# Token operands moved by 128 and 64 bytes in SBUF, a mask moved into the gates, two evacuations on another engine, one norm half a step earlier

## The chip, the cores and the metric

One core of one Trainium2 chip runs the whole program. The time is the device time of one execution in microseconds (us). Of three runs of the kernel before, the median is 1212.23 us (1207.42 to 1212.49). Engines are named as the profile names them: PE is TensorE's matrix multiply, PEld its weight load, DVE is VectorE, ACT is ScalarE, POOL is GpSimd, SP is SyncE, which here only issues DMAs.

## The reference, cut to what matters

A trunk of two layers on 512 tokens with 1024 channels, in float32. Each layer is a token mixer and a feed-forward network (FFN), each behind an RMS norm and added to the residual. The mixer of layer 0 is a convolution module, that of layer 1 a sparse attention with three branches per head.

```python
for i in range(2):
    h = rmsnorm(x, norm_mix[i])
    y = conformer_conv_module(h, ...) if i == 0 else nsa_attention(h, positions, ...)
    x = x + y
    h = rmsnorm(x, norm_ffn[i])
    gate, up = split(h @ w_in, 2)                 # 1024 -> 2 x 2816
    x = x + (silu(gate) * up) @ w_out             # 2816 -> 1024
```

In the attention the first branch looks at 31 compressed blocks of 32 tokens, the second at selected blocks (with 512 tokens all eight blocks are selected), the third at a window. Each branch's result is multiplied by a sigmoid gate:

```python
s_c = q @ k_cmp.T * scale
p_c = masked_softmax(s_c, cmp_end <= t)           # softmax of where(mask, s, -1e30), times mask
...
return g[0] * (p_c @ v_cmp) + g[1] * o_s + g[2] * o_w
```

Tokens 0 to 30 come before the end of the first compressed block: their whole row of `mask` is false, so `p_c` is zero there.

## The kernel before

Channels lie on the 128 partitions, tokens along the free axis, in tiles of 128 x 512. Each large product is made in float32r from halves: a float32 operand is split into a rounded high half and the rest, and high times high, high times low and low times high are added up in PSUM. A weight unit of 128 x 1024 comes by DMA into `wr`, ACT copies it to `wh`, DVE subtracts to `wl`. Names ending in h and l are such halves. In the profile nearly all instructions carry L136, the line of the helper that records them, so they are told apart by tile names.

The stages in order of time: conv module, first matmuls `pp<-hh,wh`, a convolution partly on PE (`cpe`) and partly on DVE, and an output product `pp<-a,wh` with the token tiles `a`; FFN of layer 0; projections, scores and outputs of the attention, ending in `pp<-oh,wh` and `pp<-ol,wh`; FFN of layer 1.

**The FFN.** The first channels are plain products of 512 columns. For the other 17 pairs of gate and up tiles per layer (function `pair`) the kernel uses seven products of half size in place of eight (Strassen's scheme in Winograd's form): `operand` combines the token tiles into `bh` and `bl` once, and for each pair the weights are combined: POOL starts two DMAs per pair into `S` (the second adds while it writes), adds `wr` to it, and `s_part` splits the sums into `sh` and `sl`. `product` then runs 4 x 3 matmuls with 256 columns each: the weights (`wh`, `wl`, `sh`, `sl`) are loaded into PE, the token half `bh` or `bl` streams. So a pair is 84 matmuls, and all pairs are 2 x 17 x 84 = 2856. The output product is `st<-ah,wh` and its like, with 512 columns.

**Where tiles lie.** Pools on the left side of SBUF are stacked upwards, those opened with `side="right"` downwards, so a small tile put on the right moves all right tiles that are opened after it. `EDGE` (24 floats) and `APART` (16 floats) are such tiles. By the addresses of the built program, the streamed tile starts this far from the weights that it meets, modulo 256 bytes: 64 for `pp<-hh` and `pp<-hl`, `st<-ah` and `st<-al`, `st<-bh` and `st<-bl`, and `pp<-oh`; 128 for `pp<-ol`; 192 for `pp<-a`. In `pv<-wh,hh` the roles are exchanged: the tokens `hh` are loaded as weights and `wh` or `wl` streams; there the distance is 192, with 256 or 304 columns.

**The attention.** `v_half(1, ...)` makes the window branch's values, four groups of 128 tokens in two PSUM banks, beside the first scores; `v_evac` copies them to SBUF, scaled by each token's norm. Then 16 steps follow (8 head pairs, two branches each). A step computes eight score tiles `S` (PE), their row maximum with the causal mask (DVE, `Pm,mx<-S`), the exponential and its sum (ACT), divides and multiplies by the gate (`weigh` on POOL, `Pm<-Pm,sm,gates`), transposes the result of the step before (`T`, PE, copied to `t` by DVE or ACT), and multiplies the one before that with the values (`O`). PE, DVE and ACT run in the order written here; for work that belongs beside the steps, the table `FILL` names what is run in each step's middle and end (`run_fill`, two entries a step; `+` joins several). `P1.0` to `P1.5` are the compressed branch's six parts for one pair of heads: `soft_a` (maximum, subtraction, exponential of the scores `sc`), `soft_b`, `soft_c` (row sum `cl`, its reciprocal, times the gate, times `sc`), `trans` (transposes to `pct`). The first pair's parts stand in `V_BESIDE` instead, beside the `pv` products. `n4` to `n7` multiply a query tile `qraw` by its norm, which PE spreads over the partitions (`bc<-qys,er`) in a PSUM bank of the same pool of three as `T` and `pct`.

Of the kernel before, what the change touches and what calls it, by code (L numbers as in the profile page):

```python
# [10 lines left out]
F32 = mybir.dt.float32  # L11
# [4 lines left out]
ALU = mybir.AluOpType  # L16
# [3 lines left out]
P = 128  # L20
T = 512
D = 1024
NK = 8
# [3 lines left out]
TAPS = 31  # L27
# [16 lines left out]
C_CMUL = C_CADD + 256  # L44
# [43 lines left out]
}  # L88
V_BESIDE = (
    (("w r12", "st0", "p2m", "sABCD a1"), ("w sa sb", "t1", "r13 c1", ""), ("w", "", "", "")),  # L90
    (("ga", "w", "s0", "s1 b1"), ("", "s2 s3 w", "gb s4 l", "s5 st1"), ("s6 l", "s7 l", "sc cu", "")))
EVAC_V = ((1, 3), (1, 3))
V_BANK = (2, 3, 0, 1)
STK_P = (0,)

FILL = ("tr0 P1.0  P1.1 P1.2  P1.3 P1.4  - n4+P1.5+d3  k3+P2.0 n5  P2.1+d5 P2.2  P2.3 P2.4  k5 P2.5  n6 n7+P3.0  "
        "P3.1 P3.2  P3.3 P3.4  wd P3.5  w0 -  w1").split()
SQB = 4
Q2B = 4
# [9 lines left out]
OUT_N = 256  # L109
EDGE = 24  # L110
APART = 16


def _two_pi_pieces():
# [34 lines left out]
def trunk(ctx: ExitStack, tc: tile.TileContext, A, out):  # L149
    order = [False]  # L150
    nc = Engines(tc, order)
# [9 lines left out]
    def nm(s):  # L161
        cnt[0] += 1
        return f"{s}_{cnt[0]}"
# [30 lines left out]
    for z in QV_ORDER:  # L194
        if z < 8:
            add("nw_q", z, 1024)
        else:
            w = VW[z - 8]
# [77 lines left out]
    cx0 = ExitStack()  # L276
    cb = cx0.enter_context(tc.tile_pool(name="cb", bufs=1, side="right"))
    ph = cb.tile([P, NPH], F32, name="ph")
    wdw = cb.tile([P, NK * TAPS + EDGE], F32, name="wdw")[:, :NK * TAPS]
    wtab = cb.tile([P, len(PE_CONV) - LOADED, 320], F32, name="wtab")  # L280
    i16 = cb.tile([P, 16], F32, name="i16")
    cc = cst.tile([P, NCST], F32, name="cc")
# [503 lines left out]
    def ffn(acc, gnext, layer, between=None):  # L786
# [9 lines left out]
        with ExitStack() as cx:  # L796
# [2 lines left out]
            pm = cx.enter_context(tc.tile_pool(name="fpm", bufs=6, space=PSUM, reuse_waits="tile"))  # L799
            pa = cx.enter_context(tc.tile_pool(name="fpa", bufs=2, space=PSUM, reuse_waits="tile"))  # L800
            sx = ExitStack()
            sb = sx.enter_context(tc.tile_pool(name="sb", bufs=1, side="right", reuse_waits="tile"))
            sx.enter_context(tc.tile_pool(name="apart", bufs=1, side="right")).tile([P, APART], F32, name=nm("apart"))
            sw = sx.enter_context(tc.tile_pool(name="sw", bufs=1, side="right", reuse_waits="tile"))
            box = {}

# [123 lines left out]
            def bank():  # L930
                return pm.tile([P, T], F32, tag="pm", name=nm("st"))
# [82 lines left out]
            pss, w, ws = {0: bank()}, {0: next_w(False)}, {}  # L1014
# [41 lines left out]
            for m, b in OUT_ORDER[4:]:  # L1056
# [12 lines left out]
                else:  # L1069
                    n = OUT_N if m == NK - 1 else T  # L1070
# [32 lines left out]
    def nsa(acc, cosT, sinT, gnext):  # L1103
        cx = ExitStack()

        def pool(cxx, name, bufs, **kw):
            return cxx.enter_context(tc.tile_pool(name=name, bufs=bufs, **kw))
# [81 lines left out]
        sx = ExitStack()  # L1189
# [199 lines left out]
        def q_pair(p):  # L1389

            a = p // 2
            sc = qk.tile([P, 4, 2, 64], F32, tag="sc", name=nm("sc"), bufs=1)

            def move(jj):
                q = oT[2 * p + jj]
                box["q2", jj] = []
                for par in range(2):
                    hs = slice(par * 64, par * 64 + 64)
                    q2 = qk.tile([P, T], F32, tag="q2", name=nm("q2"), bufs=Q2B)
                    for half in range(2):  # L1400
                        nc.sync.dma_start(q2[half * 64:half * 64 + 64], q[hs])
                    box["q2", jj].append(q2)

            def stacks(jj):
                j = 2 * p + jj
                S2 = qk.tile([P, 1088], F32R, tag="S", name=nm("St"), bufs=3)
                for par in range(2):
                    ls = slice(64 - par * 64, 128 - par * 64)
                    q2 = box["q2", jj][par]
                    S = S2[:, par * T:par * T + T]  # L1410
                    if p > 0 and par in STK_P:
                        nc.gpsimd.tensor_copy(S, q2)
                        nc.gpsimd.tensor_tensor(S[ls], q2[ls], S[ls], ALU.subtract)
                    else:
                        nc.scalar.activation(S, q2, AF.Copy)
                        behind(lambda S=S, q2=q2, ls=ls: nc.vector.tensor_tensor(S[ls], q2[ls], S[ls], ALU.subtract))
                    qst[j, par] = S

            def scores(jj):
                q = oT[2 * p + jj]  # L1420
                ps = p2.tile([P, 4, 64], F32, tag="p2", name=nm("psc"))
                for t in range(4):
                    pe(nc.tensor.matmul(ps[:, t, :], q[:, t * P:(t + 1) * P], kcb[a], start=True, stop=True))
                nc.vector.scalar_tensor_tensor(
                    sc[:, :, jj, :], ps, -1.0,
                    cc[:, C_CADD:C_CADD + 256].rearrange("p (t n) -> p t n", t=4), ALU.mult, ALU.add)

            def soft_a():
                s3 = sc.rearrange("p t j (h n) -> p (t j h) n", h=2)
                m = qk.tile([P, 16 + APART], F32, tag="cm", name=nm("cm"), bufs=1)[:, :16]  # L1430
                nc.vector.tensor_reduce(m, s3, AX.X, ALU.max)
                nc.vector.tensor_tensor(s3, s3, m.unsqueeze(2).to_broadcast([P, 16, 32]), ALU.subtract)
                sf = sc.rearrange("p t j n -> p (t j n)")
                behind(lambda: nc.scalar.activation(sf, sf, AF.Exp))

            def soft_b():
                s5 = sc.rearrange("p t j (h n) -> p t (j h) n", h=2)
                nc.gpsimd.tensor_tensor(
                    s5, s5, cc[:, C_CMUL:C_CMUL + 128].rearrange("p (t n) -> p t n", t=4)
                    .unsqueeze(2).to_broadcast([P, 4, 4, 32]), ALU.mult)  # L1440

            def soft_c():
                s3 = sc.rearrange("p t j (h n) -> p (t j h) n", h=2)
                l = qk.tile([P, 16], F32, tag="cl", name=nm("cl"), bufs=1)
                nc.vector.tensor_reduce(l, s3, AX.X, ALU.add)
                nc.vector.tensor_scalar(l, l, 0.5, None, ALU.max)
                nc.vector.reciprocal(l, l)
                r0 = 2 * (p % 2)
                gv = gates[:, :, 8 * a:8 * a + 8].rearrange("p t (h r) -> p t r h", h=2)[:, :, r0:r0 + 2, :]
                lv = l.rearrange("p (t j h) -> p t j h", t=4, j=2)  # L1450
                nc.vector.tensor_tensor(lv, lv, gv, ALU.mult)
                nc.gpsimd.tensor_tensor(
                    s3, s3, l.unsqueeze(2).to_broadcast([P, 16, 32]), ALU.mult)

            def trans():
                pt = p2.tile([P, T], F32, tag="p2", name=nm("pct"))
                for t in range(4):
                    pe(nc.tensor.transpose(pt[:, t * P:(t + 1) * P], sc[:, t].rearrange("p j n -> p (j n)"), ident))
                ph = q3[1].tile([P, T], F32R, tag="pch", name=nm("pch"))
                pl = q3[1].tile([P, T], F32R, tag="pcl", name=nm("pcl"))  # L1460
                nc.scalar.activation(ph, pt, AF.Copy)
                behind(lambda: nc.vector.tensor_tensor(pl, pt, ph, ALU.subtract))
                pcT[p] = (ph, pl)

            if p == 0:
                return move, scores, stacks, soft_a, soft_b, soft_c, trans
            return [lambda: (move(0), scores(0)), lambda: (stacks(0), scores(1)), lambda: (move(1), soft_a()),
                    lambda: (stacks(1), soft_b()), soft_c, trans]

        extra, bcs = {}, {}  # L1470

# [55 lines left out]
            extra[(f"q{j}", f"n{j}")[j > 3]] = lambda e=j + 6: (norm_mm(e), norm_x(e))  # L1527

        def first_pair():
            move, scores, stacks, soft_a, soft_b, soft_c, trans = q_pair(0)  # L1530
            extra.update(p0=lambda: scores(0), p1=lambda: scores(1), st0=lambda: stacks(0), st1=lambda: stacks(1),
                         p2m=lambda: move(1), sa=soft_a, sb=soft_b, sc=soft_c, tr0=trans)
            move(0)

        extra["m0q"] = first_pair
# [7 lines left out]
        for e in range(2, 14):  # L1543
# [7 lines left out]
            n = state["next"]  # L1551
# [18 lines left out]
        gates = ap_.tile([P, 4, 48], F32, name="gates")  # L1570
# [15 lines left out]
        def v_evac(hf, pst):  # L1586
            br = 1 + hf
            z = vf[br] = ap_.tile([P, 4, 256], F32, tag="w1v", name=f"v{br}", bufs=2)
            for t in range(4):
                ps = pst[t]  # L1590
                r1 = rt[:, t:t + 1]
                if t in EVAC_V[hf]:
                    nc.vector.tensor_scalar(z[:, t], ps[:, :256], r1, None, ALU.mult)
# [19 lines left out]
        def sigm_b():  # L1613
            g2 = gates.rearrange("p a b -> p (a b)")
            nc.vector.tensor_scalar(g2, g2, 1.0, None, ALU.add)
            nc.vector.reciprocal(g2, g2)

        extra["ga"] = sigm_a
        extra["gb"] = sigm_b
# [116 lines left out]
        N = len(us)  # L1736
        fill_ = list(FILL)
        U = {}
# [37 lines left out]
        pS.append(pool(ax, "apS2", 1, space=PSUM, **rw))  # L1776
        pO = pool(ax, "apO", 1, space=PSUM, **rw)
        ox = ExitStack()
        oha = pool(ox, "oha", 1, side="right", **rw)
        q3.append(pool(ax, "q3", 2, **rw))  # L1780
        box["q4"] = pool(ax, "q4", 2, **rw)
# [227 lines left out]
```

## Time and profile before

| | us |
|---|---|
| three runs: median, lowest, highest | 1212.23, 1207.42, 1212.49 |
| the profiled execution, its own time | 1214.0 |
| its span on the core | 1212.2 |
| PE busy in the span | 1192.2 |
| DVE, ACT, POOL busy | 791.0, 562.4, 369.9 |
| bytes moved by DMA | 154.25 MB |

The granted TensorE clock is 0.998 of full speed over the span. Matmuls are pipelined: a record of a matmul lasts longer than the distance to the next start, so a busy share near 1 says that PE's queue never ran dry, not how dense it ran. Below, the pitch of matmuls is taken from start to start. A bracket at a row's end gives the idle time of the engine before it and what ended it.

### The profile page before, as it was taken

What the parts mean: (1) busy time and instruction counts of PE and PEld (TensorE: products, weight loads), DVE (VectorE), ACT (ScalarE), POOL (GpSimd) and SP (SyncE); (2) the same over time, 40 slices, a digit from 0 to 9 for tenths busy, and PEclk for the clock granted to TensorE, in tenths of its full rate; (3) what the DMA queues carried; (4) which work ended last, traced back from release to release, by engine and by line L of the source; (5) the groups of instructions that cost most, each with busy time, mean ns of one, the idle gap of its engine ahead of it and who ended that gap; (6) DMA issues with size and microseconds to landing.
All of it is one profiled execution on the core that took longest, in us unless ns stands there. A gap on an engine that the chain in (4) does not pass through costs nothing.

```text
span 1212.2 us, 20771 instructions
## 1 busy us (share of the span) xinstructions
PE 1192.2 (98%) x8015; PEld 1022.9 (84%) x8015; DVE 791.0 (65%) x1453; ACT 562.4 (46%) x1048; POOL 369.9 (31%) x403
## 2 busy tenths in 40 slices
PE   9999899999999999999999999999999999999998
PEld 7888678799999988888779776778879999998887
DVE  7879686877776555334677778764597766656221
ACT  6212454455555443233335687773355555554111
POOL 1039022144443201102221577752213444410000
PEclk9999999999999999999999999999999999999999
DMA  9635326367777133244254211012626777723331
GB/s 363 251 107 141 80 90 198 112 157 183 185 188 178 59 105 96 97 146 113 80 140 125 52 37 36 18 36 85 181 100 160 186 192 187 181 75 99 113 114 44
DMA packets 81539, 154.25 MB, mean 127 GB/s; under 512 B 36128, under 2 KB 37024, under 8 KB 80672
## 3 DMA queue, kind: packets, MB, share of 16 engines
q1 hardware_dynamic: 66096, 109.04, 29.4%
q0 software_dynamic: 15344, 43.88, 15.3%
q8 instruction: 63, 1.03, 0.4%
q14 instruction: 36, 0.29, 0.1%
HBM read 139.37 MB, written 5.28 MB: 119 GB/s over the span
## 4 chain that ended last, share of the span: by engine, by line
PE 90%; DVE 5%; ACT 2%; issue 1%; POOL 1%; DVEq 0%; ACTq 0%
PE st L136 47%; PE pp L136 29%; PE cpe L136 2%; PE O L136 2%; PE S L136 2%; PE pv L136 2%; PE T L136 2%; ACT Pm L136 1%; DVE Pm L136 1%; DVE c L136 1%; POOL Pm L136 1%; DVE t L136 1%; DVE St L136 0%; PE psc L136 0%; DVE a L136 0%
## 5 line engine op out<-in xcount | busy, mean ns | idle before, releaser
L136 ACT ACTIVATE wh<-wr 128x1024 fp32r<-128x1024 f32 (+3 forms) x158 | 160.5, 1016 | 294.5 <-PE st L136 140.2
L136 DVE TENSOR_TENSOR wl<-wr,wh 128x1024 fp32r<-128x1024 f32 (+3 forms) x158 | 185.4, 1173 | 129.6 <-ACT wh L136 129.4
L136 PE MATMUL st<-bh,sl 128*128 128x256 f32 x680 | 190.3, 280 | 1.1 <-DVE sl L136 1.1
L136 PE MATMUL st<-bl,sh 128*128 128x256 f32 x680 | 190.1, 279 | 0.0
L136 PE MATMUL st<-bh,sh 128*128 128x256 f32 x680 | 189.7, 279 | 0.0
L136 PE MATMUL pp<-hh,wh 128*128 128x512 f32 x416 | 166.0, 399 | 1.6 <-ACT wh L136 1.0
L136 PE MATMUL pp<-hh,wl 128*128 128x512 f32 x416 | 163.2, 393 | 0.0
L136 PE MATMUL pp<-hl,wh 128*128 128x512 f32 x416 | 162.9, 392 | 0.0
L136 PE MATMUL st<-ah,wh 128*128 128x512 f32 x352 | 138.3, 393 | 0.0
L136 PE MATMUL st<-al,wh 128*128 128x512 f32 x352 | 137.7, 391 | 0.0
L136 PE MATMUL st<-ah,wl 128*128 128x512 f32 x352 | 137.3, 390 | 0.0
L136 PEld LDWEIGHTS st<-bh,sl 128*128 128x128 f32 x680 | 127.4, 187 | 1.5 <-DVE sl L136 1.5
L136 PEld LDWEIGHTS st<-bl,sh 128*128 128x128 f32 x680 | 127.8, 188 | 0.1
L136 PEld LDWEIGHTS st<-bh,sh 128*128 128x128 f32 x680 | 127.5, 188 | 0.1
L136 POOL TENSOR_TENSOR S<-S,wr 128x512 f32<-128x512 f32 x68 | 94.7, 1393 | 95.7 <-DMA wr<-fw_in 69.9
L136 POOL DMA_DIRECT2D S<-fw_x x68 | 60.4, 889 | 174.2 <-DVE sl L136 132.4
L136 DVE TENSOR_TENSOR sl<-S,sh 128x512 fp32r<-128x512 f32 x136 | 89.9, 703 | 33.4 <-ACT sh L136 33.3
L136 POOL TENSOR_SCALAR Pm<-Pm,sm,gates 128x512 f32<-128x512 f32 (+3 forms) x128 | 84.0, 670 | 49.8 <-DVE sm L136 31.5
L136 PEld LDWEIGHTS pp<-hh,wh 128*128 128x128 f32 x416 | 78.3, 188 | 23.2 <-issue 3.7
L136 PEld LDWEIGHTS pp<-hl,wh 128*128 128x128 f32 x416 | 78.3, 188 | 17.2 <-DVE hl L136 0.4
L136 PEld LDWEIGHTS pp<-hh,wl 128*128 128x128 f32 x416 | 78.2, 188 | 17.1 <-DVE wl L136 0.3
L136 POOL TENSOR_TENSOR acc<-acc,sq 128x512 f32<-128x512 f32 x18 | 31.7, 1763 | 192.4 <-ACT sq L136 179.0
(256 smaller groups left out, 2460.0 us busy)
## 6 DMA issues: line engine op xcount, KB each, us to landing
S<-fw_x POOLq DMA_DIRECT2D x68, 512.0 KB, 6.0
wr<-fw_in SPq DMA_DIRECT2D x46, 512.0 KB
wr<-fw_o SPq DMA_DIRECT2D x32, 512.0 KB
r<-fw_x SPq DMA_DIRECT2D x34, 256.0 KB
bd<-bands POOLq DMA_DIRECT2D x6, 1280.0 KB, 18.4
wr<-cw_in SPq DMA_DIRECT2D x14, 512.0 KB
wr<-fw_o SPq DMA_DIRECT2D x16, 384.0 KB
wr<-fw_s SPq DMA_DIRECT2D x8, 512.0 KB
```

The source lines that it names most:

```text
L136: z = f(*a, **kw)
```

## The change

Four edits. No constant of the computation differs.

1. Three spacers. `ASIDE` (32 floats) is put behind `wdw`, ahead of the FFN's pool of `bh` and `bl`, and added to the spacer behind that pool, so that `S`, `sh` and `sl` move by 256 bytes; 16 floats stand ahead of `oha`, the pool of `ol`. By the built addresses the distance modulo 256 bytes is now 192 for all 2856 matmuls that stream `bh` or `bl` (64 before), 64 for the 192 that stream `a` (192 before), and 64 for the 64 that stream `ol` (128 before). All other large products keep theirs.
2. `soft_b`, the product of `sc` with the mask on POOL, is gone, and so is the lower bound of 0.5 on the row sum `cl`. In their place one product multiplies the compressed branch's 16 gates of each token by the mask's first column, once.
3. `EVAC_V`: the second half's four evacuations `v<-pv` are all on ACT; two of them were on DVE.
4. `FILL`: `n4` moves from the end of step 4 to its middle, whose entry was empty.

```diff
-    (("w r12", "st0", "p2m", "sABCD a1"), ("w sa sb", "t1", "r13 c1", ""), ("w", "", "", "")),
+    (("w r12", "st0", "p2m", "sABCD a1"), ("w sa", "t1", "r13 c1", ""), ("w", "", "", "")),
...
-EVAC_V = ((1, 3), (1, 3))
+EVAC_V = ((1, 3), ())
...
-FILL = ("tr0 P1.0  P1.1 P1.2  P1.3 P1.4  - n4+P1.5+d3  ...
+FILL = ("tr0 P1.0  P1.1 P1.2  P1.3 P1.4  n4 P1.5+d3  ...
...
+ASIDE = 32
...
-    wdw = cb.tile([P, NK * TAPS + EDGE], F32, name="wdw")[:, :NK * TAPS]
+    wdw = cb.tile([P, NK * TAPS + EDGE + ASIDE], F32, name="wdw")[:, :NK * TAPS]
...
+            sx.enter_context(tc.tile_pool(name="aside", bufs=1, side="right")).tile([P, ASIDE], F32, name=nm("aside"))
             sb = sx.enter_context(tc.tile_pool(name="sb", bufs=1, side="right", reuse_waits="tile"))
-            ... .tile([P, APART], F32, name=nm("apart"))
+            ... .tile([P, APART + ASIDE], F32, name=nm("apart"))
...
-            def soft_b():
-                s5 = sc.rearrange("p t j (h n) -> p t (j h) n", h=2)
-                nc.gpsimd.tensor_tensor(
-                    s5, s5, cc[:, C_CMUL:C_CMUL + 128].rearrange("p (t n) -> p t n", t=4)
-                    .unsqueeze(2).to_broadcast([P, 4, 4, 32]), ALU.mult)
...
                 nc.vector.tensor_reduce(l, s3, AX.X, ALU.add)
-                nc.vector.tensor_scalar(l, l, 0.5, None, ALU.max)
                 nc.vector.reciprocal(l, l)
...
             nc.vector.reciprocal(g2, g2)
+            some = cc[:, C_CMUL:C_CMUL + 128].rearrange("p (t n) -> p t n", t=4)[:, :, :1]
+            nc.vector.tensor_tensor(gates[:, :, :16], gates[:, :, :16], some.to_broadcast([P, 4, 16]), ALU.mult)
...
+        pool(ox, "aside", 1, side="right").tile([P, APART], F32, name="aside")
         oha = pool(ox, "oha", 1, side="right", **rw)
```

How the instructions stand now, at three places. On DVE at the end of the value products, before the change (`cl` is `soft_c`'s row sum of the first pair, `St` a split of queries, `v` an evacuation, `Pm,mx` the row maximum of a score tile of step 1):

```order
L136 TENSOR_REDUCE cl_6938<-sc_6453 128x16
L136 TENSOR_SCALAR cl_6938<-cl_6938 128x16
L136 RECIPROCAL cl_6938<-cl_6938 128x16
L136 TENSOR_TENSOR cl_6938<-cl_6938,gates 128x16
L136 TENSOR_TENSOR St_6896<-q_643_6615,St_6896 64x512
L136 TENSOR_TENSOR St_6896<-q_644_6618,St_6896 64x512
L136 TENSOR_SCALAR v_6958<-pv_6773,rsy_5621 128x256
L136 TENSOR_SCALAR v_6958<-pv_6774,rsy_5621 128x256
L136 ISA Pm_6981,mx_6982<-S_6987,mask 128x512
```

and after:

```order
L137 TENSOR_REDUCE cl_6943<-sc_6458 128x16
L137 RECIPROCAL cl_6943<-cl_6943 128x16
L137 TENSOR_TENSOR cl_6943<-cl_6943,gates 128x16
L137 TENSOR_TENSOR St_6901<-q_644_6620,St_6901 64x512
L137 TENSOR_TENSOR St_6901<-q_645_6623,St_6901 64x512
L137 ISA Pm_6989,mx_6990<-S_6995,mask 128x512
L137 ISA mx_6990 128x1
```

The bound on `cl` (its TENSOR_SCALAR) and both evacuations `v` are gone from between the row sum and step 1's first maximum. On ACT there, two rows `v` became four, in the same place ahead of step 1's first exponential. On POOL in step 3, where the part `P1.3` of the second pair runs, before:

```order
L136 CAST St_7266<-q_726_7198 128x512
L136 TENSOR_TENSOR St_7266<-q_726_7198,St_7266 64x512
L136 TENSOR_TENSOR sc_7069<-sc_7069,cc 128x512
L136 TENSOR_SCALAR Pm_7221<-Pm_7221,sm_7223,gates 128x512
L136 TENSOR_SCALAR Pm_7221<-Pm_7221,sm_7223,gates 128x384
L136 TENSOR_SCALAR Pm_7221<-Pm_7221,sm_7223,gates 128x256
L136 TENSOR_SCALAR Pm_7221<-Pm_7221,sm_7223,gates 128x128
```

and after:

```order
L137 CAST St_7274<-q_727_7206 128x512
L137 TENSOR_TENSOR St_7274<-q_727_7206,St_7274 64x512
L137 TENSOR_SCALAR Pm_7229<-Pm_7229,sm_7231,gates 128x512
L137 TENSOR_SCALAR Pm_7229<-Pm_7229,sm_7231,gates 128x384
L137 TENSOR_SCALAR Pm_7229<-Pm_7229,sm_7231,gates 128x256
L137 TENSOR_SCALAR Pm_7229<-Pm_7229,sm_7231,gates 128x128
```

The product `sc<-sc,cc` no longer stands between the split of queries and the first weighing; the same happens in the two later pairs. On PE in step 4 before, the middle,

```order
L136 MATMUL T_7379<-cc,Pm_7221 128x128 x2
L136 MATMUL T_7379<-cc,Pm_7224 128x128 x2
L136 MATMUL T_7387<-cc,Pm_7221 128x128 x4
L136 MATMUL S_7397<-kst_6267,St_7144 128x512
L136 MATMUL S_7397<-kl_6268,St_7144 128x512
L136 MATMUL T_7402<-cc,Pm_7224 128x128 x4
```

and the end of the step:

```order
L136 MATMUL S_7422<-kst_6267,St_7144 128x256
L136 MATMUL S_7422<-kl_6268,St_7144 128x256
L136 MATMUL bc_7430<-qys_6825,er 128x512
L136 MATMUL pct_7433<-cc,sc_7069 128x128 x4
L136 MATMUL T_7447<-cc,Pm_7221 128x128 x4
L136 MATMUL T_7454<-cc,Pm_7224 128x128 x4
```

After, the middle of it:

```order
L137 MATMUL T_7385<-cc,Pm_7229 128x128 x2
L137 MATMUL T_7385<-cc,Pm_7232 128x128 x2
L137 MATMUL bc_7393<-qys_6829,er 128x512
L137 MATMUL T_7396<-cc,Pm_7229 128x128 x4
L137 MATMUL S_7406<-kst_6272,St_7152 128x512
L137 MATMUL S_7406<-kl_6273,St_7152 128x512
L137 MATMUL T_7411<-cc,Pm_7232 128x128 x4
```

`bc` now stands between the first four transposes of the step and the next four; on DVE its reader `qraw<-qraw,bc` moves with it, from behind the step's last maximum to ahead of the copy `t<-T` in the middle. Everything else stands in the order it had.

More of the change, by code (lines that the diff above doesn't have):

```diff
@@ L89 @@
 V_BESIDE = (
-    (("w r12", "st0", "p2m", "sABCD a1"), ("w sa sb", "t1", "r13 c1", ""), ("w", "", "", "")),
+    (("w r12", "st0", "p2m", "sABCD a1"), ("w sa", "t1", "r13 c1", ""), ("w", "", "", "")),
     (("ga", "w", "s0", "s1 b1"), ("", "s2 s3 w", "gb s4 l", "s5 st1"), ("s6 l", "s7 l", "sc cu", "")))
-EVAC_V = ((1, 3), (1, 3))
+EVAC_V = ((1, 3), ())
 V_BANK = (2, 3, 0, 1)
 STK_P = (0,)
-FILL = ("tr0 P1.0  P1.1 P1.2  P1.3 P1.4  - n4+P1.5+d3  k3+P2.0 n5  P2.1+d5 P2.2  P2.3 P2.4  k5 P2.5  n6 n7+P3.0  "
+FILL = ("tr0 P1.0  P1.1 P1.2  P1.3 P1.4  n4 P1.5+d3  k3+P2.0 n5  P2.1+d5 P2.2  P2.3 P2.4  k5 P2.5  n6 n7+P3.0  "
         "P3.1 P3.2  P3.3 P3.4  wd P3.5  w0 -  w1").split()
@@ L801, in ffn @@
             sx = ExitStack()
+            sx.enter_context(tc.tile_pool(name="aside", bufs=1, side="right")).tile([P, ASIDE], F32, name=nm("aside"))
             sb = sx.enter_context(tc.tile_pool(name="sb", bufs=1, side="right", reuse_waits="tile"))
-            sx.enter_context(tc.tile_pool(name="apart", bufs=1, side="right")).tile([P, APART], F32, name=nm("apart"))
+            sx.enter_context(tc.tile_pool(name="apart", bufs=1, side="right")).tile([P, APART + ASIDE], F32, name=nm("apart"))
             sw = sx.enter_context(tc.tile_pool(name="sw", bufs=1, side="right", reuse_waits="tile"))
@@ L1465, in q_pair @@
             if p == 0:
-                return move, scores, stacks, soft_a, soft_b, soft_c, trans
+                return move, scores, stacks, soft_a, soft_c, trans
             return [lambda: (move(0), scores(0)), lambda: (stacks(0), scores(1)), lambda: (move(1), soft_a()),
-                    lambda: (stacks(1), soft_b()), soft_c, trans]
+                    lambda: stacks(1), soft_c, trans]
         extra, bcs = {}, {}
@@ L1529, in first_pair @@
         def first_pair():
-            move, scores, stacks, soft_a, soft_b, soft_c, trans = q_pair(0)
+            move, scores, stacks, soft_a, soft_c, trans = q_pair(0)
             extra.update(p0=lambda: scores(0), p1=lambda: scores(1), st0=lambda: stacks(0), st1=lambda: stacks(1),
-                         p2m=lambda: move(1), sa=soft_a, sb=soft_b, sc=soft_c, tr0=trans)
+                         p2m=lambda: move(1), sa=soft_a, sc=soft_c, tr0=trans)
             move(0)
```

## The prediction

> **What bounds the kernel now.** I read the page's totals first, then the chain that ended last, then the costliest groups with their shapes, and then, since PE is never idle for long, the distances between matmul starts in the timeline of PE.
>
> ```profile
> span 1212.2 us, 20771 instructions
> PE 1192.2 (98%) x8015; PEld 1022.9 (84%) x8015; DVE 791.0 (65%) x1453; ACT 562.4 (46%) x1048; POOL 369.9 (31%) x403
> PE 90%; DVE 5%; ACT 2%; issue 1%; POOL 1%; DVEq 0%; ACTq 0%
> ```
>
> PE is busy for 98% of the span and 90% of the last chain. So only two things can move the time: how densely PE's matmuls follow each other, and the few places where PE waits.
>
> The groups that the change touches by address, and how often each occurs:
>
> ```profile
> L136 PE MATMUL st<-bh,sl 128*128 128x256 f32 x680 | 190.3, 280 | 1.1 <-DVE sl L136 1.1
> ...
> L136 PE MATMUL st<-bh,wl 128*128 128x256 f32 x272 | 76.0, 279 | 0.0
> ...
> L136 PE MATMUL pp<-a,wl 128*128 128x512 f32 x64 | 24.8, 395 | 0.0
> ```
>
> Three groups of 680 and three of 272 stream `bh` or `bl`: 2856. Their mean of 280 ns is longer than the distance to the next start, so it tells nothing of density; the pitch does. In the timeline of PE I took a stretch of each kind without a gap, its first and its last row:
>
> ```profile
> 320.84 0.28 PE L136 MATMUL st<-bh,sh 128*128 128x256 f32 x1
> ...
> 338.97 0.28 PE L136 MATMUL st<-bl,sh 128*128 128x256 f32 x1
> ...
> 660.12 0.28 PE L136 MATMUL pv<-wh,hl 128*128 128x256 f32 x1
> ...
> 661.48 0.28 PE L136 MATMUL pv<-wh,hl 128*128 128x256 f32 x1
> ...
> 461.66 0.39 PE L136 MATMUL st<-ah,wl 128*128 128x512 f32 x1
> ...
> 479.97 0.39 PE L136 MATMUL st<-al,wh 128*128 128x512 f32 x1
> ...
> 166.02 0.40 PE L136 MATMUL pp<-a,wl 128*128 128x512 f32 x1
> ...
> 181.42 0.40 PE L136 MATMUL pp<-a,wl 128*128 128x512 f32 x1
> ...
> 831.82 0.40 PE L136 MATMUL pp<-oh,wh 128*128 128x512 f32 x1
> ...
> 849.94 0.40 PE L136 MATMUL pp<-oh,wh 128*128 128x512 f32 x1
> ```
>
> With the starts counted between them, the pitches are:
> - `st<-bh` and kin, 256 columns, distance 64: 18.13 us over 154 starts, 117.7 ns;
> - `pv`, 256 columns, distance 192: 1.36 us over 12 starts, 113.3 ns;
> - `st<-ah` and kin, 512 columns, distance 64: 18.31 us over 80 starts, 228.9 ns;
> - `pp<-a`, 512 columns, distance 192: 15.40 us over 66 starts, 233.3 ns;
> - `pp<-oh` and `pp<-ol`, 512 columns, 64 and 128: 18.12 us over 78 starts, 232.3 ns.
>
> All five run at full clock with a weight load before every matmul. What differs is the place of their tiles: 512 columns do best at 64, 256 columns at 192.
>
> **The products in the FFN.** 2856 matmuls go from 64 to 192. The nearest row is `pv`: same 256 columns, same float32r, same order of two matmuls with one weight and a third with another, at 192. If the products take its pitch, each saves 117.7 - 113.3 = 4.4 ns, and all 2856 x 4.4 ns = 12.6 us. The other end comes from the 512 columns, where 192 is slower than 64 by 233.3 - 228.9 = 4.4 ns: 12.6 us lost. I take the gain, since its row has the same width and the same distance, while the other shares only the distance.
>
> The Trainium skill ("SBUF — State Buffer", section "Who interferes with whom") says that PE has two independent read ports, one for the streamed operand and one for weight loads, and that only the port pair shared by VectorE and GpSimd causes contention. By that rule the products would stay at 117.7 ns and this term would be zero; the pitches of `pp<-a` and `st<-ah`, 233.3 and 228.9 ns for the same shape, speak against it.
>
> **The two products of 512 columns.** `pp<-a` comes to 64: 192 x (233.3 - 228.9) = 0.8 us. `pp<-oh` and `pp<-ol` come to 64 throughout: 192 x (232.3 - 228.9) = 0.7 us. Together 1.5 us, with ends 0 and 1.5. The `cpe` matmuls stream `uf` against `bd`, which move together; a dozen more matmuls of the layer norm change their distance and are too few to count.
>
> **Does the FFN's supply keep up?** A pair of 84 products shrinks from 9.9 to 9.5 us. PE's wait for `sl` above is 1.1 us over the whole kernel. The transfers in the middle of the stage:
>
> ```profile
> core 0: us, PE busy (x) PEld busy (x) DVE busy (x) ACT busy (x), PEclk, DMA share, GB/s
> 300.00:340.00 40.00, 40.00 (x342) 40.00 (x341) 6.96 (x17) 4.53 (x12) 1.00 0.76 187
> ```
>
> The DMA engines are busy for 0.76; at the new pace it would be 0.79. I take no loss.
>
> **The end of the value products.** DVE, PE and ACT there:
>
> ```profile
> 672.68 0.54 DVE L136 TENSOR_SCALAR cl<-cl 128x16 f32<-128x16 f32 x1
> 673.89 2.14 DVE L136 TENSOR_TENSOR St<-q,St 64x512 fp32r<-64x512 f32 x2
> 675.96 0.86 DVE L136 TENSOR_SCALAR v<-pv,rsy 128x256 f32<-128x256 f32 x2
> 676.48 0.39 PE L136 MATMUL S<-kst,St 128*128 128x256 f32 x1 [1.97 <-DVE v L136]
> 677.48 0.39 PE L136 MATMUL S<-kst,St 128*128 128x256 f32 x1 [0.48 <-DVE mx L136]
> ...
> 673.74 0.48 ACT L136 ACTIVATE v<-pv,rsy 128x256 f32<-128x256 f32 x1 [0.22 <-PE pv L136]
> 677.46 0.72 ACT L136 ACTIVATE Pm<-Pm,mx 128x512 f32<-128x512 f32 x1 [3.24 <-DVE mx L136]
> ```
>
> PE waits 1.97 us until DVE has emptied a bank of `pv` behind two long splits, and then 0.48 us for the first row maximum. With all four on ACT the bank is free at about 674.2, ahead of PE's need; ACT's two more pieces of 0.48 us lie in its idle 3.24. Then the maximum is late next: DVE still does `St` first, but without the bound (0.54) and the two `v` (0.86), which overlap their neighbours a little, it comes 1.3 us earlier. So the gain is 1.3 us; the ends are 0, if the first exponential or its sum is late instead, and 2.45 (both waits). The added product on the gates is of the size of the other small ones on `gates`, some 0.25 us, once, and DVE idles longer just behind it:
>
> ```profile
> 667.54 0.25 DVE L136 TENSOR_SCALAR gates<-gates 128x192 f32<-128x192 f32 x1
> ...
> 670.75 0.42 DVE L136 CUSTOM_DVE_ANT_0 Pm<-S,mask 128x256 f32<-128x256 f32 x1 [0.48 <-PE S L136]
> ```
>
> **`soft_b`.** Four instructions on POOL. The first pair's lies in the value products, where PE does not wait for it. The other three look alike; this is the first of them, POOL and then PE and DVE:
>
> ```profile
> 700.76 1.29 POOL L136 TENSOR_TENSOR sc<-sc,cc 128x512 f32<-128x512 f32 x1
> 702.04 4.32 POOL L136 TENSOR_SCALAR Pm<-Pm,sm,gates 128x512 f32<-128x512 f32 x6
> ...
> 706.41 0.87 PE L136 MATMUL T<-cc,Pm 128*128 128x128 f32 x6 [0.58 <-POOL Pm L136]
> 707.97 0.66 PE L136 MATMUL T<-cc,Pm 128*128 128x128 f32 x4 [0.21 <-POOL Pm L136]
> ...
> 711.56 0.63 PE L136 MATMUL T<-cc,Pm 128*128 128x128 f32 x4 [0.99 <-DVE qraw L136]
> ...
> 707.33 0.69 DVE L136 COPY t<-T 128x512 f32<-128x512 f32 x1 [0.77 <-PE T L136]
> ...
> 710.74 0.67 DVE L136 TENSOR_TENSOR qraw<-qraw,bc 128x512 f32<-128x512 f32 x1
> ...
> PE T L136 <- POOL Pm L136: 2.3, 6, 0.6
> ```
>
> POOL runs without a gap from 700.76 on, and PE's transposes wait for it twice, 0.58 and 0.21 us; the last row (from the list of PE's waits between 640 and 800) gives 2.3 us for six such waits in all three places. 1.29 us less on POOL is more than either wait, so all 2.3 go; DVE idles 0.77 for the same cause and follows. Ends: 0, if DVE or ACT holds PE at the same places, and 3 x 1.29 = 3.9.
>
> **`n4`.** The wait of 0.99 us at 711.56 is for a PSUM bank that `bc` holds until DVE comes to `qraw`. In the step's middle that product (0.67 us) falls into DVE's idle 0.77 us, which edit 2 also shrinks, so part of it now delays the copy `t`. I take 0.7 us; ends -0.67 (all of it delays the copy and PE behind it) and 0.99.
>
> **The sum.** 12.6 + 1.5 + 1.3 + 2.3 + 0.7 = 18.4 us, 12.6 of it in the products. Against the profiled execution's own 1214.0 (span 1212.2) that is 1195.6; the median of the runs, 1212.23, lies 1.8 lower and would give 1193.8. I name 1195.
>
> **Rivals.**
> - The distance means nothing at 256 columns and `pv` is quicker for another reason: the small groups it runs in or the exchanged roles of tokens and weights. For it: the stretch is short, 12 starts against 154. Against it: `pp<-a` and `st<-ah` show that places matter. Then 1.5 + 1.3 + 2.3 + 0.7 = 5.8 us remain: 1206.4. The skill's rule of independent ports leads here too, and without the 1.5 us: 1207.9.
> - 192 is a bad distance for any stream, as 512 columns show: 2856 x 4.4 ns lost, less the other 5.8: 1212.2 + 12.6 - 5.8 = 1219. Against it stands the whole `pv` stretch. It decides from a pitch of 117.7 + 5800/2856 = 119.7 ns upwards, where the kernel gets slower than before.
> - The products' supply gets late, because 17 pairs in a row ask for more transfers per time; DMA, at 0.76, holds the pairs halfway. 6.3 us of the 12.6 are lost: 1200 to 1201.
>
> **How the numbers follow.** The sum 0.74, no effect at 256 columns 0.12, worse at 192 0.08, late supply 0.06. A measurement of this kernel can tell about 0.5%, 6 us: the first and the last are faster (0.80), the second is within it (0.12), the third slower (0.08). For the range, the sum's own lower end is 12.6 + 1.5 + 2.45 + 3.9 + 0.99 = 21.4, 1190.8 from the median, and 1189 with what single runs lie lower; upwards it takes in the late supply and the rival without effect, to 1208, which leaves out the slower rival and a little of each edge.
>
> **What the profile after would show.** Products right: the pitch of `st<-bh` in the middle of a pair near 113.3 ns, 154 starts in 17.5 us in place of 18.1, `pp<-a` and `pp<-oh` at 228.9. Supply wrong: idle before `st<-bh,sl` or `st<-bh,wh` above a few us, ended by DVE `sl` or `wl`. Evacuation right: no PE wait on `v` ahead of step 1, and the first `mx` 1.3 us earlier. `soft_b` right: PE's waits on POOL `Pm` gone. `n4` right: no PE wait on `qraw` in step 4, and no new one of that length on `t` or `pch`. The forecast is wrong if the pitch of the products stays at 117.7 or rises; no other term is large enough to save it.

## The result, and the profile after

The changed kernel takes 1202.52 us (median of 18 runs, 1195.52 to 1210.15) against 1213.15 us before (18 runs, 1205.91 to 1215.02): a ratio of the means of 0.9932, with a 95% interval from 0.9911 to 0.9954. By that interval it is faster by 5.6 to 10.8 us, where 18.4 us were worked out. The profiled execution took 1201.69 us. Three lines of its page, to be held against those of before:

```profile
span 1199.9 us, 20754 instructions
PE 1182.6 (99%) x8015; PEld 1015.9 (85%) x8015; DVE 794.6 (66%) x1448; ACT 562.1 (47%) x1050; POOL 363.4 (30%) x399
PE 92%; DVE 4%; ACT 2%; issue 1%; DMA 0%; SPq 0%; DVEq 0%; ACTq 0%
```

PE still bounds the kernel, and POOL has left the chain. From matmul start to matmul start, the two profiled executions differ by stage like this (us):

| stage | before | after | difference | forecast |
|---|---|---|---|---|
| `pp<-a`, first to last | 47.19 | 46.40 | -0.79 | -0.8 |
| products of the FFN, layer 0 | 171.62 | 171.61 | -0.01 | -6.3 |
| attention, last `pv` to last `O` | 141.76 | 136.88 | -4.89 | -4.3 |
| `pp<-oh`, `pp<-ol`, first to last | 44.44 | 43.83 | -0.61 | -0.7 |
| products of the FFN, layer 1 | 171.63 | 165.49 | -6.14 | -6.3 |

All other stages agree within 0.04 us, and the span is 12.3 us shorter. So one of two equal layers gained everything that was forecast for it and the other nothing. Two windows of 40 us, one in the products of layer 0 and one in those of layer 1, show it, first of before and then of after. The columns are the window, its length, PE's busy time with the number of matmuls `st` in it, the granted clock, the DMA share and GB/s.

```profile
320.00:360.00 40.00, 40.00 (x342) 1.00 0.77 189
1000.00:1040.00 40.00, 40.00 (x342) 1.00 0.76 186
```

```profile
320.00:360.00 40.00, 40.00 (x342) 1.00 0.75 188
1000.00:1040.00 40.00, 40.00 (x355) 1.00 0.79 194
```

A matmul of 0.28 us counts if any part of it lies in the window, so the pitch is (40 + 0.28)/n: 117.8 ns for 342 and 113.5 ns for 355. From the starts themselves it is 117.8 and 113.3 ns, and nothing between. Layer 0 runs at the one and layer 1 at the other, with the same code, the same distance of 192 and full clock in both. The timeline of PE after shows where the two layers part. These are the first wait for `sl` in layer 0 and in layer 1:

```profile
247.66 0.28 PE L137 MATMUL st<-bl,sh 128*128 128x256 f32 x1
248.47 0.39 PE L137 MATMUL st<-bh,sl 128*128 128x256 f32 x1 [0.54 <-DVE sl L137]
248.70 0.28 PE L137 MATMUL st<-bh,sh 128*128 128x256 f32 x1
...
249.52 0.28 PE L137 MATMUL st<-bl,sh 128*128 128x256 f32 x1
...
913.59 0.28 PE L137 MATMUL st<-bl,sh 128*128 128x256 f32 x1
914.41 0.39 PE L137 MATMUL st<-bh,sl 128*128 128x256 f32 x1 [0.53 <-DVE sl L137]
914.63 0.28 PE L137 MATMUL st<-bh,sh 128*128 128x256 f32 x1
...
915.44 0.28 PE L137 MATMUL st<-bl,sh 128*128 128x256 f32 x1
```

Both layers come into the wait at 117 to 118 ns. Seven starts after 248.70 layer 0 is at 249.52, 117 ns each. In layer 1 the single distances behind the wait are 222, 118, 122, 116, 114, 113 and then 113 to 114 ns: the faster pitch sets in within five matmuls of the wait. It holds for 93 distances, then comes a single one of 171 ns, and behind that it holds for 1307 more, up to twelve matmuls of 512 columns near the layer's end. This led to the theory that was tested: **the stream has two steady pitches, each interruption of PE chooses one, and the choice holds until the next interruption.** Its rivals were that the distance alone sets the pitch, and that something in layer 0 (its transfers, its weights) holds it back.

PE's waits in the attention after (640 to 800 us; total, times, longest) are those of before without `Pm` and `v`; `mx` has grown from 0.5 to 2.0 and `kl` from 0.5 to 0.9, and one on `sm` is new:

```profile
PE S L137 <- DVE mx L137: 2.0, 1, 2.0
PE T L137 <- DVE qraw L137: 1.0, 2, 0.7
PE S L137 <- DVE kl L137: 0.9, 1, 0.9
PE T L137 <- DVE sm L137: 0.4, 1, 0.4
```

### The profile page after: what moved, and what is told of

Its sections match the earlier page's. It is cut to its first block, busy times and chain, and to the rows that moved or that the text cites. A ratio compares the mean times of both kernels' runs of the same rounds, so it can differ in the third digit from the quotient of the medians.

```text
span 1199.9 us, 20754 instructions
## 1 busy us (share of the span) xinstructions
PE 1182.6 (99%) x8015; PEld 1015.9 (85%) x8015; DVE 794.6 (66%) x1448; ACT 562.1 (47%) x1050; POOL 363.4 (30%) x399
## 4 chain that ended last, share of the span: by engine, by line
PE 92%; DVE 4%; ACT 2%; issue 1%; DMA 0%; SPq 0%; DVEq 0%; ACTq 0%
PE st L137 47%; PE pp L137 29%; PE O L137 3%; PE S L137 3%; PE T L137 3%; PE cpe L137 2%; PE pv L137 2%; DVE c L137 1%; ACT Pm L137 1%; DVE Pm L137 1%; PE psc L137 0%; DMA x<-xT 0%; DVE a L137 0%; ACT wh L137 0%; ACT sh L137 0%
```

## The experiments

Pitches are means of start-to-start distances within a stretch; "fast" means 113.3 to 113.5 ns, "slow" 117.7 to 117.8 ns.

**The other edits without the spacers.**

```diff
-ASIDE = 32
 # both spacers of ASIDE and the one ahead of oha taken out
```

> Edits 2 to 4 without the spacers: distances 64, 192 and 128 as before the change. Theory lock (products run at 117.7 or 113.3 ns, chosen in each layer when PE comes out of its stall in the first pair and kept from there on; the distance only shifts the odds): times lie on levels 6.2 us apart, some 4.9 us under those of the kernel before: near 1208.5 with no layer fast, 1202.3 with one. Theory address alone (the distance sets the pitch, and layer 0 of the changed kernel is held at 117.7 by something of that layer): one level, 1208 to 1209, and no 113.3 anywhere in the products. Either way the stretch from the value products' end to the last O matmul is 136.9 us, as in the changed kernel, and pp<-a takes 47.2.

Measured: 1210.02 us (6 runs, 1208.55 to 1211.75) against 1213.67 (18 runs), ratio 0.997, interval 0.9958 to 0.9981. `pp<-a` and the output product are back at 47.20 and 44.46 us. Both layers run slow at distance 64, 171.6 us each, but layer 0 did not begin so. The timeline of PE in this kernel, the first and the 13th product, the next one and the wait:

```profile
246.77 0.28 PE L137 MATMUL st<-bh,wh 128*128 128x256 f32 x1
...
248.13 0.28 PE L137 MATMUL st<-bh,sh 128*128 128x256 f32 x1
248.24 0.28 PE L137 MATMUL st<-bl,sh 128*128 128x256 f32 x1
249.12 0.38 PE L137 MATMUL st<-bh,sl 128*128 128x256 f32 x1 [0.59 <-DVE sl L137]
```

From 246.77 to 248.13 are 12 distances of 113.3 ns, at 64 bytes. Behind the wait come 1401 distances of 117.8 ns on average, without a break. So the fast pitch exists at the old place too, and the wait ended it.

**The spacers alone.**

```diff
+ASIDE = 32
 # the three spacers of edit 1; edits 2, 3 and 4 undone
```

> The spacers alone, edits 2 to 4 undone: distances 192, 64, 64. Theory lock: levels near 1212, 1206 and 1199.5 (no, one or two layers fast), more often fast than the kernel before. Theory address alone: always layer 1 fast and layer 0 slow, one level near 1206. Either way pp<-a takes 46.4 and the oh products 43.8 us, and the stretch from the value products' end to the last O matmul is 141.8 us.

Measured: 1211.1 us (12 runs, 1205.5 to 1214.42) against 1213.67, ratio 0.997, interval 0.9955 to 0.9985. `pp<-a` gains 0.70 and the output product 0.61 us. In the profiled execution (1213.42 us) each layer runs fast for 93 matmuls behind the wait for `sl`, until, some 108 products into the layer, a distance of 166 ns (167 in layer 1) appears; from there on it is slow. The timeline there, with PE's weight loads (PEld) and ACT:

```profile
259.82 0.64 ACT L137 ACTIVATE c<-st 128x256 f32<-128x256 f32 x2
...
260.07 0.19 PEld L137 LDWEIGHTS st<-bh,sl 128*128 128x128 f32 x1
260.18 0.28 PE L137 MATMUL st<-bh,sl 128*128 128x256 f32 x1
260.23 0.19 PEld L137 LDWEIGHTS st<-bh,sh 128*128 128x128 f32 x1
260.29 0.33 PE L137 MATMUL st<-bh,sh 128*128 128x256 f32 x1
...
260.46 0.28 PE L137 MATMUL st<-bl,sh 128*128 128x256 f32 x1
```

An interruption of some 50 ns is enough. It is a wait for ACT, too short to be noted in a bracket: the product at 260.29 adds to a PSUM tile that ACT copies to `c` first, and the first of the two copies ends at 260.18. The load of that product's weights starts 57 ns after the matmul before it, where others start 2 to 5 ns after. In all 13 profiled executions whose first pair has the wait for `sl`, that copy starts 10.3 us behind the product that waited, at either pitch. A slow stream (17 layers) comes to the place 0.36 to 0.39 us after the copy has ended and shows no gap; a fast one (9 layers) comes 0.4 us earlier and has to wait, in each of the nine. Of these nine, seven were slow from there on (distances of 159 to 174 ns), and two stayed fast: layer 1 of the changed kernel (171 ns) and one at 64 bytes (193 ns). The times of the 12 runs, from 1205.5 to 1214.42, scatter by more than one layer's 6.2 us.

**Added interruptions.** In the next four kernels and two later ones, a matmul of another width, called a kick here, is put into the stream, once in two pairs or, in one kernel, in each of the first three. Its result goes to a spare PSUM tile and is used by nothing; the computation is otherwise complete.

```diff
+KICK = ((0, 512, 0, 448, 0, 384, 0, 352, 0, 320, 0, 304, 0, 288, 0, 272, 0),
+        (0, 480, 0, 416, 0, 368, 0, 336, 0, 312, 0, 296, 0, 280, 0, 264, 0))
...
                 product(b, w1, 1, 1, True, True)
+                if KICK[layer][n]:
+                    z = pa.tile([P, T], F32, tag="pa", name=nm("kick"))
+                    pe(nc.tensor.matmul(z[:, :KICK[layer][n]], w1[0][:, :P], bh[0][:, :KICK[layer][n]],
+                                        start=True, stop=True))
```

With 16 widths in the changed kernel (distance 192):

> The changed kernel with one extra matmul of another width (264 to 512 columns, its result unused) in the middle of every second pair of products, 16 in all. Theory lock: some of the 16 flip the pitch of all that follows between 117.7 and 113.3, both ways possible, and the pitch is the same within each stretch between two of them, in layer 0 too. Theory address alone: the pitch returns to the layer's own value (117.7 in layer 0, 113.3 in layer 1) behind each. The extra matmuls themselves cost 16 x 0.16 = 2.6 us.

The same 16 widths with the three spacers taken out (distance 64):

> The same 16 extra matmuls, spacers undone (distance 64). Theory lock: stretches at 113.3 appear at 64 as well, fewer or as many as at 192. Theory address alone: 117.7 in all stretches.

Measured: 1203.27 and 1211.78 us (one run each). Every stretch of 168 matmuls between two kicks has one pitch throughout. Windows of 18 us, now (18 + 0.28)/n: 161 or 162 is fast, 155 or 156 slow. First three stretches of layer 0 at 192 (behind 512, 448 and 384 columns):

```profile
262.20:280.20 18.00, 18.00 (x161) 1.00 0.79 202
281.50:299.50 18.00, 18.00 (x156) 1.00 0.80 205
301.50:319.50 18.00, 18.00 (x161) 1.00 0.83 203
```

and three of layer 1 at 64 (behind 368, 336 and 312 columns):

```profile
973.30:991.30 18.00, 18.00 (x161) 1.00 0.78 202
992.50:1010.50 18.00, 18.00 (x155) 1.00 0.76 205
1012.50:1030.50 18.00, 18.00 (x162) 1.00 0.78 202
```

At 192, 10 of 16 stretches are fast (behind 512, 384, 320, 304, 288, 272 in layer 0, and 416, 368, 312, 264 in layer 1); at 64, 2 of 16 (behind 368 and 312). Counted only where the stream was slow ahead of the kick, these are 6 of 8 and 2 of 14. Both layers have fast and slow stretches at 192, within the same supply, so neither the layer nor the transfers hold the pitch down; and both pitches occur at both distances, so the distance alone does not set it.

**One width again and again, at 192.** Layer 0 and layer 1 get these tables:

```diff
+KICK = ((0, 304, 0, 304, ...), (0, 320, 0, 320, ...))
```

> The changed kernel with an extra matmul of 304 columns in every second pair of layer 0 and of 320 in layer 1, eight each. Theory lock with a fixed outcome by width: as 304 and 320 columns both ended at 113.3 ns in the run with mixed widths, all 16 stretches behind them do, and the products take 2 x 162.5 us. Rival, lock with chance at each interruption: both pitches behind one and the same width, about 10 of 16 fast.

```diff
+KICK = ((0, 512, 0, 512, ...), (0, 288, 0, 288, ...))
```

> The same with 512 columns in layer 0 and 288 in layer 1. Fixed outcome by width: all 16 stretches at 113.3 ns. Fixed outcome by width and by the pitch before: 288 (fast to fast with mixed widths) keeps the state it finds fast, 512 (slow to fast) may alternate. Chance: about 10 of 16 fast, in no order.

Measured: 1208.29 and 1202.41 us (one run each; one run of before on that chip took 1214.8). Neither outcome written down for 304 and 320 came, all fast or a mixture without order. A kick of 304 left the slow stream slow 8 times of 8 (with mixed widths it had left a fast one fast). 320 and 512 change the pitch every time: fast, slow, fast, slow, 8 times of 8 each. Behind 288 the stream is fast 8 times of 8, the first time coming from the slow pitch. Windows with 512, two of layer 0, then with 288, two of layer 1:

```profile
263.40:281.40 18.00, 18.00 (x161) 1.00 0.80 210
282.70:300.70 18.00, 18.00 (x156) 1.00 0.82 204
...
928.20:946.20 18.00, 18.00 (x161) 1.00 0.82 204
947.40:965.40 18.00, 18.00 (x161) 1.00 0.80 204
```

So for kicks the outcome is no lottery: one width does the same each time, given the pitch before it. For 304 the pitch before is shown to matter, since the sixth kick of layer 0 left a fast stream fast in one kernel and a slow one slow in the other. For 320 and 512 the pitch before and the kick's place in the order (every second one) go together and were not separated. The natural interruptions vary a little: the distance over the wait for `sl` is 811 to 817 ns at 192 bytes, 812 to 815 where the stream came out fast and 811 to 817 where it came out slow. That this is why their outcome varies is argued and not shown.

**Edits 2, 3 and 4, each alone on the kernel before.**

```diff
 # edit 2: the mask multiplied into the gates; soft_b and the bound on cl gone
-                nc.vector.tensor_scalar(l, l, 0.5, None, ALU.max)
+            nc.vector.tensor_tensor(gates[:, :, :16], gates[:, :, :16], some.to_broadcast([P, 4, 16]), ALU.mult)
```

> Edit 2 alone (mask in the gates, no soft_b), everything else as before the change. By the prediction's step the stretch from the value products' end to the last O matmul, 141.8 us before, shortens by 2.3, and PE's waits on POOL Pm, 2.3 us, are gone. Rival, that DVE or ACT holds PE at the same places: under 1 us.

```diff
-EVAC_V = ((1, 3), (1, 3))
+EVAC_V = ((1, 3), ())
```

> Edit 3 alone (all four evacuations of the second half on ACT). By the prediction's step the same stretch shortens by 0.8 us (the bound on cl, worth 0.5 of the 1.3, stays here), PE's wait on DVE v of 2.0 is gone, and one on DVE mx of about 1.7 stands in its place. Rival, that the first exponential is late instead: 0.

```diff
-FILL = ("tr0 P1.0  P1.1 P1.2  P1.3 P1.4  - n4+P1.5+d3  ...
+FILL = ("tr0 P1.0  P1.1 P1.2  P1.3 P1.4  n4 P1.5+d3  ...
```

> Edit 4 alone (n4 in step 4's middle). By the prediction's step the stretch from the value products' end to the last O matmul, 141.8 us before, shortens by 0.7 and PE's waits on DVE qraw fall from 1.7 to 0.7 us. Rival, that the norm on DVE delays the copy t for POOL-bound transposes: 0 or slightly longer.

Measured, one run each: 1210.81, 1213.0 and 1206.49 us, against 1214.8, 1214.8 and 1213.18 before; the attention changes by -3.25, -1.94 and -0.89 us. PE's waits in it move as the prediction says: with edit 2 alone those on `Pm` are gone and `v` stays,

```profile
PE S L137 <- DVE v L137: 2.1, 1, 2.1
PE T L137 <- DVE qraw L137: 1.9, 2, 1.1
```

with edit 3 alone `v` is gone and `mx` takes its place,

```profile
PE T L136 <- POOL Pm L136: 2.4, 6, 0.6
PE S L136 <- DVE mx L136: 1.9, 1, 1.9
```

and with edit 4 alone `qraw` falls from 1.7 in two waits to 0.7 in one. But the three alone add up to 6.1 us, and together they gave 4.89 in the changed kernel and 3.54 without the spacers. Following the scores `S` of the 16 steps, start by start against before, shows why. The differences arise at four places only: the end of the value products and the compressed branch of pairs 1, 2 and 3. (In us; each column is one profiled execution.)

| place | edit 2 | edit 3 | edit 4 | all three, no spacers | after |
|---|---|---|---|---|---|
| end of `pv`: 4th score tile | +0.09 | -0.78 | -0.03 | -0.71 | -0.69 |
| from there to the 7th | -1.16 | -1.15 | +0.38 | +0.30 | -1.16 |
| pair 1 | -0.81 | +0.02 | -1.20 | -1.68 | -1.65 |
| pair 2 | -0.48 | +0.02 | 0.00 | -0.50 | -0.49 |
| pair 3 | -0.88 | -0.04 | -0.05 | -0.95 | -0.90 |

The second row is no work of any edit. Windows of 2 us on PE in before, in the kernel without spacers and in after show it in the column behind the bracket, the granted clock:

```profile
678.00:680.00 2.00, 2.00 (x13) 0.62 0.19 42
680.00:682.00 2.00, 1.98 (x8) 0.53 0.00 0
```

```profile
678.00:680.00 2.00, 2.00 (x11) 0.50 0.55 125
680.00:682.00 2.00, 1.78 (x11) 0.75 0.00 0
```

```profile
678.00:680.00 2.00, 1.59 (x12) 1.00 0.00 0
680.00:682.00 2.00, 2.00 (x20) 1.00 0.00 0
```

Behind PE's wait of about 2 us the clock falls to half for 3.4 us in some executions (in the first two windows 0.38 and 0.47 of 2 us each are missing, 1.7 us in all, which is 3.4 us at half the clock), and that costs 1.2 to 1.5 us. Of the nine profiled executions that contain edits 2 to 4, it happened in four, and the `mx` wait of 2.0 to 2.1 us ahead of it stands in all nine. Their attention gained 3.54 to 4.22 us against before, that of the other five 4.89 to 5.39. Of the kernels without all three edits, before, the spacers alone and edit 4 alone have it, edits 2 and 3 alone don't. The clock records of the traces show what decides. Every trace also has a halving at its end, behind the last matmuls, and in all seven that have the one in question it starts 155 or 156 steps of 3.413 us ahead of that last one and lasts one step. Counted on this grid, PE stood idle for 1.9 to 2.3 us of the step just before the halving; in the seven traces without it, the step with most idle time around the wait has 1.1 to 1.9 us. So a wait of 2 us halves the clock where nearly all of it falls into one step, and not where a line of the grid divides it; the two groups touch at 1.9 us. The Trainium skill ("TensorE: Matmul & The Clock Gate", section "What's actually happening") says that the clock is halved after an idle window of about 3.4 us, and that this window runs freely, so the point of change varies from run to run. The traces agree with the step of 3.413 us; they do not with a whole window of idle time, since 1.9 to 2.3 us within one step were enough.

The run with edit 4 alone told one thing more: its layer 1 runs fast, 165.42 us, at distance 64:

```profile
320.00:360.00 40.00, 40.00 (x342) 1.00 0.74 189
1000.00:1040.00 40.00, 40.00 (x356) 1.00 0.76 197
```

Its 1206.49 us lie 6.7 below before's 1213.18 on that chip, 6.2 of it in this layer. That size also fits the two levels in the 18 runs of before at the top: 6 at 1205.9 to 1208.2, 12 at 1212.2 to 1215.0. Profiles of those runs don't exist, so this is only argued.

**Setting the fast pitch early.** Three kicks of 288 columns at the start of each layer, and in the first pair a product that needs no `sl` ahead of the one that does:

```diff
+KICK = ((288, 288, 288, 0, 0, ...), (288, 288, 288, 0, 0, ...))
...
+                if n == 0:
+                    b = bank()
+                    product(b, w1, 1, 1, True, True)
...
-                b = bank()
-                product(b, w1, 1, 1, True, True)
+                if n > 0:
+                    b = bank()
+                    product(b, w1, 1, 1, True, True)
```

> The changed kernel with one extra matmul of 288 columns in each of the first three pairs of both layers, and with the first pair's products in another order (the second product of the raw weights ahead of the first that needs sl), so that PE has no stall there. Theory lock with an outcome fixed by the width (288 columns ended at 113.3 ns from both pitches, in all eight cases and in one more): both layers run at 113.3 from the second pair on in every execution; products 2 x 162.2 us less 2 x 0.8 for the stalls plus 6 x 0.13: near 1207.5 - 12.6 - 0.8 = 1194, with no second level. Rival, that the outcome also hangs on the moment of the stall or on the first pairs: levels at 1194, 1200 and 1206.

The changed kernel once more, beside it:

> The changed kernel as it is, on the same chip. Theory lock: levels near 1208, 1201.5 and 1195 (no, one, two layers fast), some runs between them where a layer changes its pitch on the way; median 1201 to 1208.

And kicks of 288 columns every second pair at distance 64:

```diff
-ASIDE = 32
+KICK = ((0, 288, 0, 288, ...), (0, 288, 0, 288, ...))
```

> Edits 2 to 4 at the old distances with an extra matmul of 288 columns in every second pair. If the width alone decides, all 16 stretches are at 113.3 ns and the distance buys nothing that 288 columns would not. If the outcome hangs on width and distance together (at 64 the mixed widths, 288 among them, left 14 of 16 at 117.7), they are at 117.7.

Measured on one chip: 1195.26 us with the early kicks (4 runs, 1194.96 to 1197.58), ratio to before 0.9854, interval 0.9837 to 0.987; 1206.53 us for the changed kernel (6 runs, 1203.27 to 1208.87), ratio 0.994, interval 0.9926 to 0.9954; 1209.8 us (one run) for the kicks at 64. With the early kicks each layer runs at 117.8 ns up to the first kick and at 113.4 behind the third. Windows in both layers:

```profile
320.00:360.00 40.00, 40.00 (x356) 1.00 0.76 196
1000.00:1040.00 40.00, 40.00 (x355) 1.00 0.75 196
```

the changed kernel on this chip:

```profile
280.00:320.00 40.00, 40.00 (x342) 1.00 0.74 190
940.00:980.00 40.00, 40.00 (x342) 1.00 0.73 187
```

and the kicks at 64:

```profile
320.00:360.00 40.00, 40.00 (x340) 1.00 0.75 185
1000.00:1040.00 40.00, 40.00 (x340) 1.00 0.74 185
```

(340 and not 342, since the window also holds two kicks.) With the early kicks both layers take 165.81 us, and all four runs lie near one level, 1 us above the 1194 that were expected. PE's wait for `sl` is gone; two distances of 0.30 and 0.26 to 0.28 us in the second pair remain, and the second and third kick come behind them. How many of the three kicks are needed was not tested. The profiled execution of the changed kernel here was fast for 93 products in each layer and then slow, 171.27 us twice, 0.35 us less than before; nearly all of its gain is that of the other terms. At 64 bytes no kick of 288 works: slow in 16 stretches of 16, each kick costing 0.13 us. At 192, counting all kernels, the stream was fast behind 288 columns 15 times of 15; in 3 of these it had been slow ahead of the kick, and at 64 it had been slow ahead of all 17. This kernel is the fastest of all that ran, 11 us below the changed one on the same chip.

## Why the prediction was right or wrong

**The products in the FFN: the step that failed.** "If the products take its pitch, each saves 117.7 - 113.3 = 4.4 ns, and all 2856 x 4.4 ns = 12.6 us" (its meaning `pv`'s). The two pitches and the 4.4 ns are right; what is wrong is that a distance has a pitch. The same products run at either pitch at either distance, as the last interruption leaves them. And "I take no loss" counted PE's wait for `sl` and the transfers only: at the faster pitch PE overtakes ACT's copy to `c`, waits some 50 ns for it, and in seven layers of nine that turned the stream slow again. In the profiled execution of after, half the term came, 6.14 us in layer 1; in the second profiled execution 0.35 us in each layer did; with the early kicks, 5.8 us in each layer. What the spacers change is how interruptions end: fast behind 10 of 16 mixed kicks at 192 against 2 of 16 at 64, behind 288 columns 15 of 15 against 0 of 17 (from the slow pitch 3 of 3 against 0 of 17), and behind the wait for `sl` in 8 of 12 layers against 1 of 14. Past ACT's copy, one layer of the 12 and one of the 14 were still fast. The 12 distances of `pv` were a true reading of a short stretch (no unbroken one there has more than 17), and the 154 distances of `st<-bh` a true reading of another stretch. In the kernel without spacers the first 13 products of layer 0 ran at 113.3 ns at the distance called slow, and that refutes the comparison.

**The rivals.** "The distance means nothing at 256 columns" put 1206.4 us; the changed kernel's second measurement, with both layers slow in its profiled execution, has 1206.53, and the first, 1202.52, lies between that and the forecast; its profiled execution shows one fast layer in one such run. Yet the rival's reason is also wrong, as the kicks show. The third rival, transfers that come late, is excluded: PE's wait for `sl` is 1.1 us as before, and the DMA share in the fast layer is the 0.79 that was worked out; so it is luck that this rival's 1200 to 1201 us lie near the 1202.52 measured, and the supplier that was late is ACT. The steady pitch never rose above 117.8 ns. By the Trainium skill's rule of independent read ports ("SBUF — State Buffer", "Who interferes with whom") the place of the operands would not matter at all; the kicks of 288 columns from the slow pitch, 3 of 3 fast against 0 of 17, say that it does, if not in the way that was forecast.

**The two products of 512 columns: right.** 0.79 and 0.61 us against 0.8 and 0.7, repeated with the spacers alone (0.70 and 0.61). This pitch is no state of the stream: `pp<-a` runs at 233.3 ns in all seven profiled executions without spacers and at 229.1 to 229.3 ns in all seven with them. The output product takes 44.26 to 44.46 us without and 43.83 to 43.84 with them.

**The end of the value products: mechanism right, term too large.** PE's wait on `v` is gone and the maximum is late next, as forecast, but the 4th score tile starts 0.69 us earlier and not 1.3 (0.78 with edit 3 alone). The 0.54 us of the bound on `cl` were counted as earned on DVE, and edit 2 alone moved this point by +0.09: they bought nothing. The traces show where they went. In all ten profiled executions with edit 2 the two DVE instructions behind the row sum take longer, `cl<-cl,gates` 0.53 to 0.57 us and the first `St<-q,St` 1.12 to 1.13 us, where the four without it have 0.32 and 0.69; why is open. The half clock stands in the trace of before (0.62 and 0.53) and has no term in the prediction; that it was absent in the profiled execution of after makes up 1.16 of the stage's 4.89 us, which is luck. Without it the stage gained 3.73 us where 4.3 were forecast.

**`soft_b`: right.** All six waits on POOL are gone; edit 2 alone gives 0.81 + 0.48 + 0.88 = 2.2 us at the three pairs against 2.3. Pair 2 gives least, and there PE waits longer for `kl` instead: 0.9 to 1.0 us where it was 0.5. In the changed kernel's second profiled execution that wait is 0.6, and pair 2 gains 0.83.

**`n4`: right.** Pair 1 gains 1.65 us with all edits, of which edit 2 alone gives 0.81; 0.84 are left for `n4` against 0.7. Alone it gave 1.20, so the two edits overlap there. The wait of 0.99 has become one of 0.24 at the new place.

## What to carry to other kernels

Take the pitch of a matmul stream from start to start, in every stretch, every layer and several executions, before a difference between two short stretches is turned into a cost per matmul: it may be a state that the stream is in and not a property of its operands. Where a stream turns out to have two steady pitches, an added matmul of the right width at its start can choose the better one (here 0.13 us each for 5.8 us per layer), but only at a placement of the operands where that width works. Where an engine is to become faster, ask of each engine that hands it something how late that already comes: ACT's copy had 0.37 us to spare, and the gain of 0.4 us used that up. And where two profiled executions are subtracted, look at the granted clock behind every wait of some 2 us first; a part of the difference may be chance.

## What the runs showed of the hardware that was not expected

- A stream of 256-column float32r matmuls, each with its weight load, runs steadily at 113.3 or 117.7 ns at full clock, for more than 1300 matmuls without a change. Interruptions from 50 ns (ACT's copy, 108 products into a layer) to 0.7 us (the wait for `sl`, a distance of 0.81 us) can switch it, and added matmuls do so repeatably: at 192 bytes 304 columns keep the pitch, 320 and 512 exchange it, 288 always ended fast.
- The place of the tiles has a share in how a given interruption ends: 288 columns from the slow pitch ended fast in 3 of 3 with the spacers and in 0 of 17 without. Only these two placements were tried, so whether it is the distance modulo 256 bytes or another property of the addresses is not shown. Why is open too: the weight load's record starts 2 to 5 ns after the start of the matmul before it at both pitches, so the records show no difference but the distance itself.
- Why ACT's copy turned seven fast streams slow and left two fast, with waits of nearly the same length, is open, and so is why the chips differed in how often a layer comes out fast.
- One wait of 2.0 us on PE halved the clock for 3.4 us in four of nine executions of the same attention code, at a price of 1.2 to 1.5 us. Over all 14 traces, the idle time within one step of a grid of 3.413 us was 1.9 to 2.3 us where the clock was halved and at most 1.1 to 1.9 us where it was not.
